# A mixer and MLP trunk on one core: adaLN transposes and ones-matmuls one step later, fewer adaLN steps in the mLSTM output gate

## The chip, the cores and the metric

The kernel runs on one core of one Trainium2 chip. The metric is device time in microseconds for one execution, the median of several. The core's engines are TensorE (PE), VectorE (DVE), ScalarE (ACT), GpSimd (POOL) and SyncE (SP), which here issues nearly all DMAs.

## What is computed

A trunk of two layers over x of 512 rows by 1024 columns, in float32. Layer 0 mixes with an mLSTM, layer 1 with a gated MLP (SGU); each mixer is followed by a squared-ReLU MLP (FFN0 and FFN1 below). Every sub-layer is wrapped by a normalisation whose scale, shift and gate come from a conditioning vector c:

```python
c_act = jax.nn.silu(c)
for i in range(DEPTH):
    mod = c_act @ ada_w[i] + ada_b[i]
    sh1, sc1, g1, sh2, sc2, g2 = jnp.split(mod[:, None, :], 6, axis=-1)
    h = rmsnorm(x, norm_g[i, 0]) * (1.0 + sc1) + sh1
    y = mlstm_mixer(...) if i % N_MIXERS == 0 else sgu_mixer(...)
    x = x + g1 * rmsnorm(y, norm_g[i, 1])
    h = rmsnorm(x, norm_g[i, 2]) * (1.0 + sc2) + sh2
    y = jnp.square(jax.nn.relu(h @ ffn_w1[i])) @ ffn_w2[i]
    x = x + g2 * rmsnorm(y, norm_g[i, 3])
```

The mLSTM computes h @ w_in into queries, keys, values, an output gate o and two gates per head; 128-row chunks then give scores (q k times a decay matrix), mixed values, a state that runs through the chunks, a head norm, and the product with sigmoid(o), which goes through w_out.

## The kernel before, in words

All large products are three float32r matmuls each: weights are loaded raw into a ring of three 16 KB-per-partition buffers (raw), ScalarE casts the high part (whi), VectorE subtracts for the low part (wlo), and `mm3` multiplies hi by hi, hi by lo and lo by hi. A unit of work is 24 such matmuls of 128x512 into one PSUM bank. The stages run in this order: q and gates, k, v (two column halves of four units, `cb`), then the output gate `o_unit` mixed with scores, keys, mixed, state and gated by a list in the code, then `out_proj` (two halves), then FFN0 and so on.

Beside this, each sub-layer prepares the adaLN numbers of its own gate g and of the next normalisation (ab) from ada_w, in small steps that the generator of `Prep` hands out: `prep.step()` stands behind most units. `ada_g` makes g in two halves s of 512 columns; each half reads two raw blocks (g1 to g4 below), sums them on VectorE into an R buffer r, casts the sum into hi and lo (buffers t), and multiplies them by a matrix of ones on TensorE into the PSUM tile pa, which sums over the partitions. `ada_ab` makes the eight column blocks of scale and shift, ab0 to ab7: two loads, two ScalarE products to begin the sums, six VectorE sums, one POOL addition that merges two partial sums (`ada_merge`), two TensorE transposes into pa (`ada_tr`), and one reduction with three small operations on VectorE (`ada_fin`). pa has one bank, R two buffers, raw three, and the weights' whi and wlo four each.

In the mLSTM, the decay matrices of two chunks at a time (`decay`) are read back from a small DRAM tensor dm by DMA, get a mask (capm) on POOL, and go through sixteen exponentials on ScalarE. Eight more reads of dm scale the queries.

Up to the q projection the instructions are kept in the program's order; after it a scheduler orders each engine's instructions by its own estimate, within what the data and the buffers allow. DMAs on SP go out in their order, and an issue whose buffer is still in use holds all behind it. A table of moved transposes (`places`, `behind`) belongs to the end of a sub-layer and is not touched. The rows carry one line number, that of the helper that records every instruction (L50), so tiles name the work. The steps concerned are:

```python
        def steps(self, gate, nxt):
            yield from ada_g(self, *gate)
            if nxt is not None:
                for k in range(KC):
                    self.ab.append(ada_ab(*nxt, k))
                    yield
```

Of the kernel before, what the change touches and what calls it, by code (L numbers as in the profile page):

```python
# [19 lines left out]
KC = D // P  # L20
# [13 lines left out]
def trunk(ctx: ExitStack, tc: tile.TileContext, x, c, norm_g, ada_w, ada_b, ffn_w1, ffn_w2,  # L34
# [62 lines left out]
    def f32(t):  # L97
        return t.bitcast(F32)
# [54 lines left out]
    def ada_load(l, vs, vc, k):  # L153
        raw = rp.tile([P, KC, 2, P], F32, tag="raw", name=nm("raw"))
        w = ada_w[l].rearrange("(k p) f -> p k f", p=P)
        for i, v in enumerate((vs, vc)):
            ld.dma_start(raw[:, :, i, :], w[:, :, v * D + k * P:v * D + (k + 1) * P])
        return raw
# [12 lines left out]
    def ada_merge(acc):  # L171
        pool.tensor_add(acc[:, 0], acc[:, 0], acc[:, 1])

    def ada_tr(acc, merge=True):
        if merge:
            ada_merge(acc)
        ps = bank3()
        for i in range(2):
            pe.transpose(out=ps[:, i * P:(i + 1) * P], in_=acc[:, 0, i * P:(i + 1) * P], identity=ident)
        return ps  # L180
# [7 lines left out]
        dve.tensor_mul(ab[:, 1:2], ab[:, 2:3], ngcol(l, ng, k))  # L188
        return ab[:, 1:2], ab[:, 0:1]

    def ada_ab(l, vs, vc, ng, k):

        raw = ada_load(l, vs, vc, k)
        acc = R().rearrange("p (c i f) -> p c (i f)", c=2, i=2)
        ada_init(raw, acc)
        ada_acc(raw, acc, range(6))
        return ada_fin(ada_tr(acc), l, vs, vc, ng, k)

    def ada_g(box, l, v, ng):

        g = gp.tile([P, D], F32, tag="g", name=nm("g"))
        box.g = g
        w = ada_w[l].rearrange("(k p) f -> p k f", p=P)
        for s in range(2):
            f0 = v * D + s * S
            acc = R()
            pool.memset(acc, 0.0)
            ld.dma_start(acc[0:1, :], ada_b[l:l + 1, f0:f0 + S])
            for hf in range(2):
                raw = rp.tile([P, 4, S], F32, tag="raw", name=nm("raw"))  # L210
                ld.dma_start(raw, w[:, hf * 4:hf * 4 + 4, f0:f0 + S])
                for j in range(4):
                    kk = hf * 4 + j
                    dve.scalar_tensor_tensor(out=acc, in0=raw[:, j], scalar=cact[:, kk:kk + 1],
                                             in1=acc, op0=ALU.mult, op1=ALU.add)
                yield
            ngb = R()
            ld.dma_start(ngb, norm_g[l, ng:ng + 1, s * S:(s + 1) * S].broadcast_to([P, S]))
            ps = bank3()
            hi, lo = T(F32R), T(F32R)  # L220
            act.copy(hi, acc)
            dve.tensor_sub(lo, acc, f32(hi))
            pe.matmul(ps, lhsT=ones, rhs=hi, start=True, stop=False)
            pe.matmul(ps, lhsT=ones, rhs=lo, start=False, stop=True)
            dve.tensor_mul(g[:, s * S:(s + 1) * S], ps, ngb)
            yield


    def conv(raw_ap, scale=None, lo_eng=None):
# [207 lines left out]
    def mlstm(h, prep, after):  # L437
# [37 lines left out]
        pt = bank2()  # L475
        for i in range(2):
            pe.transpose(out=pt[:, i * P:(i + 1) * P], in_=pk[:, i, :], identity=ident)
        aps = ada_tr(accs_[0])
        xn = []
        for t in range(NT):  # L480
# [43 lines left out]
        raws.append(ada_load(0, 0, 1, 2))  # L524
        load_q(2)
        ada_start(2)
        aps = ada_tr(accs_[1])
        xps = xT(1)
        for k in range(KC):
            if k + 2 < KC:  # L530
                ada_acc(raws[k + 2], accs_[k + 2], range(6))
            if k + 1 < KC:
                ab.append(ada_fin(aps, 0, 0, 1, 0, k + 1))
            if k + 3 < KC:
                raws.append(ada_load(0, 0, 1, k + 3))
                load_q(k + 3)
                ada_start(k + 3)
            if k + 2 < KC:
                ada_merge(accs_[k + 2])
            if k + 1 < KC:  # L540
                feed(k + 1, xps, pool)
                q_hi(k + 1)
                q_lo(k + 1)
            hh, hl = h(k, slice(0, S))
            mm3(accs[0], wgc[k // 4][0][:, k % 4], wgc[k // 4][1][:, k % 4], hh, hl, k == 0, k == KC - 1)
            for f in range(4):
                fs = slice(f * P, (f + 1) * P)
                mm3(accs[1 + f], qw[k][0][:, fs], qw[k][1][:, fs], hh, hl, k == 0, k == KC - 1)
            if k + 2 < KC:
                aps = ada_tr(accs_[k + 2], False)  # L550
                xps = xT(k + 2)
        kblk = w_cols(w, 512)
        pinned[0] = False
# [152 lines left out]
        def o_unit(cb, t):  # L706
            if t == 0:
                oblk[0] = w_rows(w, 0, 2048 + cb * S) + w_rows(w, 4, 2048 + cb * S)
            ps = bank()
            proj_tm(ps, oblk[0], h, t)  # L710
            o = A()
            act.activation(o, ps, AF.Sigmoid)
            so[t][cb] = o
            if cb or t > 1:
                prep.step()

        sts = [A(shape=(P, 2, DV + 1)) for _ in range(2)]
# [280 lines left out]
    class Prep:  # L998
# [6 lines left out]
        def steps(self, gate, nxt):  # L1005
            yield from ada_g(self, *gate)
            if nxt is not None:
                for k in range(KC):
                    self.ab.append(ada_ab(*nxt, k))
                    yield  # L1010

        def step(self, n=1):
            for _ in range(n):
# [50 lines left out]
```

## Time and profile before

| | us |
|---|---|
| median of 3 runs (1287.57 to 1288.25) | 1287.77 |
| the profiled execution | 1290.01 |
| its span on the core | 1288.3 |
| TensorE busy in the span | 1234.9 |
| VectorE / ScalarE / POOL busy | 675.9 / 523.4 / 238.7 |
| mean granted TensorE clock, of full | 0.993 |

TensorE sets the time, so one looks for the stretches in which it stands still, and for those in which it runs at the lower of its two clock levels. A timeline gives each group of instructions its start and length, and in brackets the idle time before it and the engine and tile that ended that idle time.

### The profile page before, as it was taken

The page shows a single profiled execution, that of the slowest core. Times are in us where ns is not written, and L with a number is a line of the kernel's source. Part 1 is how long each engine was busy: PE and PEld are TensorE (multiplying, and loading weights), DVE is VectorE, ACT ScalarE, POOL GpSimd, SP SyncE. Part 2 cuts the span into 40 slices and gives each one's busy share as a digit, 9 for nine tenths or more (in the row PEclk, how much of TensorE's full clock was granted, in tenths as well). Part 3 has the DMA queues.
Part 4 walks back from the last instruction along what each step waited for, and adds up shares of the span by engine and source line. Part 5 has one row for each costly group of instructions (what it writes and reads, how often), then busy time and mean ns, then how long its engine had stood idle before and what let it go on. Part 6 is the DMA issues. An engine that isn't in the chain of part 4 may idle for free.

```text
span 1288.3 us, 15197 instructions
## 1 busy us (share of the span) xinstructions
PE 1234.9 (96%) x5849; PEld 1016.5 (79%) x5849; DVE 675.9 (52%) x1124; ACT 523.4 (41%) x923; POOL 238.7 (19%) x230
## 2 busy tenths in 40 slices
PE   3899998999999999999999999999999999999997
PEld 2677777888788888888778888888887888888886
DVE  5796677476853343323786766623566222333225
ACT  4544535384433243413563644323653321343221
POOL 5601311013420022200120023200122200122000
PEclk9999999999999999999999999999999999999999
DMA  9846842424862442222367555322255214332201
GB/s 271 232 165 193 269 111 98 131 89 149 226 199 103 134 134 96 98 98 78 126 203 251 160 153 147 108 99 69 95 165 171 98 66 131 99 98 98 98 33 66
DMA packets 165610, 174.25 MB, mean 135 GB/s; under 512 B 6168, under 2 KB 120936, under 8 KB 165536
## 3 DMA queue, kind: packets, MB, share of 16 engines
q1 hardware_dynamic: 165408, 173.17, 42.8%
q8 instruction: 46, 0.75, 0.2%
q14 instruction: 28, 0.23, 0.1%
q0 software_dynamic: 128, 0.09, 0.0%
HBM read 171.11 MB, written 2.14 MB: 134 GB/s over the span
## 4 chain that ended last, share of the span: by engine, by line
PE 66%; DVE 4%; ACT 2%; POOL 1%; issue 1%; DMA 1%; DVEq 0%; POOLq 0%; ACTq 0%
PE ps L50 64%; PE pt L50 1%; POOL s L50 1%; DVE wlo L50 1%; DVE r L50 1%; DVE x L50 1%; ACT j L50 1%; DVE a L50 1%; DMA raw<-in_ada_w 1%; PE pa L50 0%; ACT whi L50 0%; ACT t L50 0%; POOL r L50 0%; DVE hlo L50 0%; DVE t L50 0%
## 5 line engine op out<-in xcount | busy, mean ns | idle before, releaser
L50 PE MATMUL ps<-whi,a 128*128 128x512 f32 x1408 | 438.5, 391 | 0.0
L50 DVE TENSOR_TENSOR wlo<-raw,whi 128x1024 fp32r<-128x1024 f32 x196 | 241.9, 1238 | 313.8 <-ACT whi L50 304.1
L50 ACT CAST whi<-raw 128x1024 fp32r<-128x1024 f32 x196 | 205.1, 1051 | 285.7 <-PE ps L50 250.2
L50 PEld LDWEIGHTS ps<-whi,a 128*128 128x128 f32 x1408 | 265.0, 188 | 54.8 <-PE pa L50 0.2
L50 PE MATMUL ps<-hlo,whi 128*128 128x512 f32 (+1 forms) x744 | 277.4, 373 | 3.0 <-POOL hlo L50 3.0
L50 PE MATMUL ps<-hhi,whi 128*128 128x512 f32 (+1 forms) x744 | 279.2, 375 | 0.6 <-ACT whi L50 0.6
L50 PE MATMUL ps<-hhi,wlo 128*128 128x512 f32 (+1 forms) x744 | 277.4, 373 | 0.7 <-DVE wlo L50 0.7
L50 PE MATMUL ps<-wlo,a 128*128 128x512 f32 x704 | 274.7, 390 | 0.0
L50 DVE SCALAR_TENSOR_TENSOR r<-raw,cact,r 128x256 f32<-128x256 f32 (+1 forms) x256 | 147.9, 617 | 29.4 <-ACT r L50 17.7
L50 PEld LDWEIGHTS ps<-hlo,whi 128*128 128x128 f32 x744 | 140.4, 189 | 28.2 <-POOL hlo L50 4.1
L50 PEld LDWEIGHTS ps<-hhi,wlo 128*128 128x128 f32 x744 | 140.3, 189 | 25.6 <-DVE wlo L50 1.5
L50 PEld LDWEIGHTS ps<-hhi,whi 128*128 128x128 f32 x744 | 140.4, 189 | 24.2 <-ACT whi L50 1.0
L50 POOL TENSOR_TENSOR t<-t 128x512 f32<-128x512 f32 x64 | 96.7, 1511 | 317.8 <-ACT t L50 317.8
L50 PEld LDWEIGHTS ps<-wlo,a 128*128 128x128 f32 x704 | 132.5, 188 | 27.0
L50 PE MATMUL ps<-wlo,hhi 128*128 128x512 f32 x256 | 101.5, 397 | 3.2 <-DVE wlo L50 3.0
L50 PE MATMUL ps<-whi,hhi 128*128 128x512 f32 x256 | 102.7, 402 | 1.3 <-ACT whi L50 1.3
L50 POOL TENSOR_TENSOR s<-s,mhalf 128x1 f32<-128x1 f32 (+1 forms) x40 | 33.9, 847 | 376.8 <-DVE s L50 369.5
L50 PE MATMUL ps<-whi,hlo 128*128 128x512 f32 x256 | 101.1, 395 | 0.4 <-DVE hlo L50 0.4
L50 DVE TENSOR_TENSOR a<-t,a 128x512 fp32r<-128x512 f32 x64 | 44.2, 691 | 75.5 <-ACT a L50 74.3
L50 ACT CAST a<-t 128x512 fp32r<-128x512 f32 x64 | 39.8, 622 | 101.6 <-POOL t L50 101.6
L50 POOL TENSOR_TENSOR r<-r 128x256 f32<-128x256 f32 x32 | 34.2, 1070 | 183.7 <-DVE r L50 142.5
L50 PEld LDWEIGHTS ps<-wlo,hhi 128*128 128x128 f32 x256 | 48.7, 190 | 15.4 <-DVE wlo L50 5.8
(128 smaller groups left out, 978.8 us busy)
## 6 DMA issues: line engine op xcount, KB each, us to landing
raw<-in_ffn_w SPq DMA_DIRECT2D x64, 1024.0 KB, 5.4
raw<-in_ada_w SPq DMA_DIRECT2D x64, 512.0 KB, 5.6
raw<-in_ada_w SPq DMA_DIRECT2D x16, 1024.0 KB, 5.1
raw<-in_b_w_in SPq DMA_DIRECT2D x16, 1024.0 KB, 5.5
raw<-in_a_w_in SPq DMA_DIRECT2D x10, 1024.0 KB, 5.2
raw<-in_b_w_out SPq DMA_DIRECT2D x8, 1024.0 KB, 6.8
raw<-in_a_w_out SPq DMA_DIRECT2D x4, 1024.0 KB, 5.1
x<-in_x SPq DMA_DIRECT2D x4, 512.0 KB, 7.5
```

The source lines that it names most:

```text
L50: r = f(*a, **k)
```

## The change

Three things are rearranged. In `ada_ab` the transposes and the final small operations of block k come in step k+1, behind the sums and the merge of block k and ahead of the loads of block k+1; it takes nine steps instead of eight. In `ada_g` the second half of the sums no longer ends a step: the cast into hi and lo stands in the same step as the sums, and the ones-matmuls open the next one; it takes four steps instead of six. And the output gate takes a step behind two of its eight units (t == 3) instead of six, so that the remaining steps fall to `out_proj`, whose first half already called `prep.step()` behind each unit.

```diff
-    def ada_tr(acc, merge=True):
-        if merge:
-            ada_merge(acc)
+    def ada_tr(acc):
         ps = bank3()
...
-    def ada_ab(l, vs, vc, ng, k):
-
-        raw = ada_load(l, vs, vc, k)
-        acc = R().rearrange("p (c i f) -> p c (i f)", c=2, i=2)
-        ada_init(raw, acc)
-        ada_acc(raw, acc, range(6))
-        return ada_fin(ada_tr(acc), l, vs, vc, ng, k)
+    def ada_ab(box, l, vs, vc, ng):
+        acc = None
+        for k in range(KC + 1):
+            ps = ada_tr(acc) if k else None
+            if k < KC:
+                raw = ada_load(l, vs, vc, k)
+                acc = R().rearrange("p (c i f) -> p c (i f)", c=2, i=2)
+                ada_init(raw, acc)
+                ada_acc(raw, acc, range(6))
+                ada_merge(acc)
+            if k:
+                box.ab.append(ada_fin(ps, l, vs, vc, ng, k - 1))
+            yield
...
-                yield
+                if hf == 0:
+                    yield
             ngb = R()
             ld.dma_start(ngb, norm_g[l, ng:ng + 1, s * S:(s + 1) * S].broadcast_to([P, S]))
-            ps = bank3()
             hi, lo = T(F32R), T(F32R)
             act.copy(hi, acc)
             dve.tensor_sub(lo, acc, f32(hi))
+            yield
+            ps = bank3()
             pe.matmul(ps, lhsT=ones, rhs=hi, start=True, stop=False)
             pe.matmul(ps, lhsT=ones, rhs=lo, start=False, stop=True)
             dve.tensor_mul(g[:, s * S:(s + 1) * S], ps, ngb)
-            yield
...
+        ada_merge(accs_[0])
         aps = ada_tr(accs_[0])
...
-            if cb or t > 1:
+            if t == 3:
                 prep.step()
...
-                for k in range(KC):
-                    self.ab.append(ada_ab(*nxt, k))
-                    yield
+                yield from ada_ab(self, *nxt)
```

The scheduler then places the DMAs and the engines' instructions anew. On SP, around the second half of the v weights, the order before is as follows. raw from in_a_w_in is a block of v weights (later of o weights), raw from in_ada_w 128x4x512 is a g block and 128x8x128 an ab block, and a from dm 128x4x128 is a decay read.

```order
L50 DMA a_1062<-dm 128x4x128
L50 DMA a_1069<-dm 128x4x128
L50 DMA a_1076<-dm 128x4x128
L50 DMA a_1083<-dm 128x4x128
L50 DMA raw_1137<-in_ada_w 128x4x512
L50 DMA r_1170<-in_norm_g 128x512
L50 DMA raw_1207<-in_ada_w 128x8x128 x2
L50 DMA raw_1256<-in_ada_w 128x8x128 x2
L50 DMA a_1278<-dm 128x4x128
L50 DMA a_1285<-dm 128x4x128
L50 DMA a_1292<-dm 128x4x128
L50 DMA a_1299<-dm 128x4x128
```

The last g block (raw_1137) and norm_g went out behind the first four decay reads, and the second four behind ab0 and ab1; the two v blocks (raw_1090, raw_1100) stood side by side nine rows further up. After the change SP has, from the same four decay reads on:

```order
L50 DMA a_1074<-dm 128x4x128
L50 DMA a_1081<-dm 128x4x128
L50 DMA a_1088<-dm 128x4x128
L50 DMA a_1095<-dm 128x4x128
L50 DMA raw_1112<-in_a_w_in 128x4x512
L50 DMA raw_1153<-in_ada_w 128x8x128 x2
L50 DMA raw_1196<-in_ada_w 128x8x128 x2
L50 DMA raw_1245<-in_ada_w 128x8x128 x2
L50 DMA raw_1294<-in_ada_w 128x8x128 x2
L50 DMA a_1313<-dm 128x4x128
L50 DMA a_1320<-dm 128x4x128
L50 DMA a_1327<-dm 128x4x128
```

The second v block (raw_1112) has the place behind the decay reads, the last g block has moved up to the others, ahead of the first v block, norm_g stands two rows ahead of the decay reads, and the second set of them comes behind two more ab blocks.

On ScalarE, at the end of the v projection, the order before the o weights' casts (whi_1329 to whi_1343) is the following; a<-a,a are the exponentials of decays 2 and 3, a<-ps the copies of v units.

```order
L50 ACTIVATE a_1292<-a_1292,a_849 128x128
L50 COPY a_858<-ps_1180 128x2x128
L50 COPY a_859<-ps_1180 128x2x128
L50 ACTIVATE a_1292<-a_1292,a_849 128x128 x3
L50 ACTIVATE a_1299<-a_1299,a_849 128x128 x4
L50 CAST whi_1329<-raw_1327 128x1024
L50 CAST whi_1333<-raw_1327 128x1024
L50 COPY a_861<-ps_1229 128x2x128
L50 COPY a_862<-ps_1229 128x2x128
L50 CAST whi_1339<-raw_1337 128x1024
L50 CAST whi_1343<-raw_1337 128x1024
```

The second pair of casts stood behind the copies of the last v unit (a_861, a_862). After the change ScalarE has, with the o weights as whi_1364 to whi_1378:

```order
L50 ACTIVATE r_1297<-raw_1294,cact 128x256 x2
L50 ACTIVATE a_1313<-a_1313,a_849 128x128 x4
L50 ACTIVATE a_1320<-a_1320,a_849 128x128 x4
L50 COPY a_861<-ps_1264 128x2x128
L50 COPY a_862<-ps_1264 128x2x128
L50 ACTIVATE a_1327<-a_1327,a_849 128x128 x4
L50 ACTIVATE a_1334<-a_1334,a_849 128x128 x4
L50 CAST whi_1364<-raw_1362 128x1024
L50 CAST whi_1368<-raw_1362 128x1024
L50 CAST whi_1374<-raw_1372 128x1024
L50 CAST whi_1378<-raw_1372 128x1024
```

The last copies of the v projection (a_861, a_862) stood behind the first o casts and now stand ahead of the last eight exponentials, and all o casts behind those.

On TensorE, the end of the second v unit (ps_1143) of this column half and the start of the third (ps_1180) before, with the second ones-matmuls of g between them:

```order
L50 MATMUL ps_1143<-whi_1106,hhi_123 128x512
L50 MATMUL ps_1143<-wlo_1107,hhi_123 128x512
L50 MATMUL ps_1143<-whi_1106,hlo_125 128x512
L50 MATMUL pa_1172<-t_1173,ones 128x512
L50 MATMUL pa_1172<-t_1174,ones 128x512
L50 MATMUL ps_1180<-whi_1092,hhi_122 128x512
```

TensorE went through the units one by one, each with the first half of the v weights (whi_1092, whi_1096) and then the second (whi_1102, whi_1106). After the change, where the second half (whi_1114, wlo_1115) is first used:

```order
L50 MATMUL ps_1215<-wlo_1109,hhi_122 128x512
L50 MATMUL ps_1215<-whi_1108,hlo_124 128x512
L50 MATMUL ps_1122<-whi_1114,hhi_123 128x512
L50 MATMUL ps_1166<-whi_1114,hhi_123 128x512
L50 MATMUL ps_1215<-whi_1108,hhi_122 128x512
L50 MATMUL ps_1215<-wlo_1109,hhi_122 128x512
L50 MATMUL ps_1215<-whi_1108,hlo_124 128x512
L50 MATMUL ps_1122<-wlo_1115,hhi_123 128x512
```

The ones-matmuls stand 19 matmuls further up. Three units now run on the first half of the weights as far as they can; before, each unit took both halves in turn.

## Rows read from the trace of the kernel before

**Rows 1.** page: busy us by engine (share of span), the chain that ended last

```profile
PE 1234.9 (96%) x5849; PEld 1016.5 (79%) x5849; DVE 675.9 (52%) x1124; ACT 523.4 (41%) x923; POOL 238.7 (19%) x230
...
PE 66%; DVE 4%; ACT 2%; POOL 1%; issue 1%; DMA 1%; DVEq 0%; POOLq 0%; ACTq 0%
```

**Rows 2.** TensorE's waits: releaser, us in total, times, longest

```profile
PE pa L50 <- POOL r L50: 8.1, 3, 5.4
...
PE pa L50 <- ACT t L50: 2.7, 1, 2.7
...
PE pa L50 <- DVE t L50: 1.1, 4, 0.5
```

**Rows 3.** timeline of TensorE, 123.6 to 128.8: start, us, operation [idle before <-releaser]

```profile
128.07 0.79 PE L50 MATMUL pa<-t,ones 128*128 128x512 f32 x1 [2.67 <-ACT t L50]
```

**Rows 4.** windows: length, busy us of each engine (instructions), granted clock, DMA share, GB/s

```profile
113.40:125.40 12.00, 12.00 (x53) 9.60 (x52) 5.39 (x8) 8.04 (x22) 6.13 (x4) 1.00 0.89 263
125.40:134.30 8.90, 6.24 (x15) 4.63 (x15) 7.57 (x17) 2.97 (x7) 0.53 (x1) 0.62 0.75 210
143.20:154.00 10.80, 9.52 (x65) 7.77 (x66) 10.61 (x20) 6.58 (x11) 0.81 (x1) 1.00 0.74 204
```

**Rows 5.** timeline of VectorE, 108 to 160

```profile
109.10 0.69 DVE L50 TENSOR_TENSOR g<-pa,r 128x512 f32<-128x512 f32 x1 [2.15 <-PE pa L50]
...
124.26 3.11 DVE L50 SCALAR_TENSOR_TENSOR r<-raw,cact,r 128x512 f32<-128x512 f32 x4 [6.58 <-DMA raw<-in_ada_w]
...
130.72 4.04 DVE L50 SCALAR_TENSOR_TENSOR r<-raw,cact,r 128x256 f32<-128x256 f32 x10
```

**Rows 6.** SP's DMA issues in time, 85 to 133

```profile
104.52 8.77 SPq L50 DMA_DIRECT2D a<-dm  x12
113.38 0.85 SPq L50 DMA_DIRECT2D raw<-in_ada_w  x1
...
126.45 4.00 SPq L50 DMA_DIRECT2D a<-dm  x4
```

**Rows 7.** page, DMA issues: KB each, median us from issue to landing

```profile
raw<-in_a_w_in SPq DMA_DIRECT2D x10, 1024.0 KB, 5.2
```

**Rows 8.** timelines of POOL (110 to 150) and ScalarE (108 to 130)

```profile
133.77 2.14 POOL L50 TENSOR_TENSOR a<-a,capm 128x512 f32<-128x512 f32 x1 [10.86 <-DMA a<-dm]
...
122.95 1.28 ACT L50 ACTIVATE a<-a,a 128x128 f32<-128x128 f32 x4 [0.32 <-POOL a L50]
```

**Rows 9.** timeline of ScalarE, 128 to 155

```profile
142.29 1.98 ACT L50 CAST whi<-raw 128x1024 fp32r<-128x1024 f32 x2
144.17 0.63 ACT L50 COPY a<-ps 128x256 f32<-128x256 f32 x2
```

**Rows 10.** timeline of TensorE, 143 to 156

```profile
150.62 0.50 PE L50 MATMUL ps<-wlo,hhi 128*128 128x512 f32 x1 [1.28 <-DVE wlo L50]
...
151.88 1.95 PE L50 MATMUL ps<-a,a 128*128 128x129 f32 x16
153.76 1.10 PE L50 MATMUL pt<-a,a 128*64 128x129 f32 x16
```

**Rows 11.** timeline of TensorE in the output gate, the rows with idle time

```profile
185.95 0.50 PE L50 MATMUL ps<-wlo,hhi 128*128 128x512 f32 x1 [1.42 <-DVE wlo L50]
...
203.52 0.63 PE L50 MATMUL pt<-ident,a 128*128 128x128 f32 x4 [0.96 <-DVE ab L50]
...
223.35 0.87 PE L50 MATMUL pt<-ident,a 128*128 128x128 f32 x3 [0.68 <-DVE ab L50]
```

**Rows 12.** timeline of TensorE in FFN0, rows of pa

```profile
339.63 0.44 PE L50 MATMUL pa<-ident,r 128*128 128x128 f32 x2 [1.44 <-POOL r L50]
...
352.66 0.44 PE L50 MATMUL pa<-ident,r 128*128 128x128 f32 x2 [1.26 <-POOL r L50]
```

**Rows 13.** FFN0: timelines of ScalarE (a unit's Relu) and VectorE (lo parts)

```profile
345.59 0.60 ACT L50 ACTIVATE t<-ps 128x512 f32<-128x512 f32 x1 [1.15 <-PE ps L50]
...
342.49 2.35 DVE L50 TENSOR_TENSOR wlo<-raw,whi 128x1024 fp32r<-128x1024 f32 x2
```

More of the change, by code (lines that the diff above doesn't have):

```diff
@@ L526, in mlstm @@
         ada_start(2)
+        ada_merge(accs_[1])
         aps = ada_tr(accs_[1])
@@ L549, in mlstm @@
             if k + 2 < KC:
-                aps = ada_tr(accs_[k + 2], False)
+                aps = ada_tr(accs_[k + 2])
                 xps = xT(k + 2)
```

## The prediction

> **What bounds the kernel now.** I read first the busy times and the chain of waits, then TensorE's waits by releaser, then the timelines of the stretches in which TensorE stands still. TensorE is busy 96% of the span and 66% of the chain that ended last is its own [rows 1]. Every matmul of before is still done, so the change can only move TensorE's idle time and its clock. The tile pa, in which the adaLN steps transpose and sum, makes it wait 8.1 us on POOL's merge of r, 2.7 us on ScalarE's t and 1.1 us on VectorE's t [rows 2]. The longest of the three POOL waits, 5.4 us, is the start-up, where the change only moves the merge call. What is at stake directly is then 2.7 + 2.7 + 1.1 = 6.5 us of idle time and what a dropped clock adds. All else is a question of what the new order of loads and casts puts in the way.
>
> **Part 1: the gate sum in the v projection (a gain).** TensorE stops at 125.4 for 2.67 us, for the second ones-matmul of g [rows 3]. Its sum is late because its last raw block, g4, is issued at 113.38, behind twelve reads of dm, and VectorE can start on it only at 124.26 [rows 5, 6]. Behind the stop the granted clock is 0.62 of full: the window of 8.90 us holds 15 matmuls, while the 12.00 us before it held 53 at clock 1.00, 0.226 us each [rows 4]. 15 x 0.226 = 3.4, so the stop costs 8.9 - 3.4 = 5.5 us, 2.7 idle and 2.8 at the half-rate level. After the change g1 to g4 are all issued ahead of the first v block of the second column half, the hi/lo is made one step ahead of its matmuls, and this cost goes: -5.5.
>
> **Part 2: the v block that gave up its place (a loss of about the same size).** The second half of those v weights (v1b) was issued with the first, well ahead; now it stands behind dm, norm_g and four decay blocks on SP's queue. norm_g waits for a buffer that VectorE's product for g frees at 109.8 [rows 5]; with it, two reads of dm and four decay reads ahead, seven issues at 0.73 us (8.77 for twelve [rows 6]), v1b goes out at about 114.9, in the place where g4 was. The nearest row is g4 itself, 10.9 us from 113.38 to 124.26; what then went out behind it, norm_g, now lies ahead, so v1b lands at 125 to 126. On ScalarE its cast stands behind the sixteen exponentials of the first two decays, whose last four began at 122.95 and took 1.28 [rows 8]; with their reads about 1.2 us later (norm_g's wait) they end at about 125.4, and the cast (1.0, as those in rows 9) at 126.5. TensorE has 33 matmuls and the ones pair to do without v1b, where it had 48 before its stop: 13 fewer x 0.226 = 2.9, so it is dry at 122.5. A stop of 4.0 us (3.4 if the reads come no later than before) and the same 2.8 us of slow clock give +6.8. Parts 1 and 2 together: +1.3, and the v stage ends at about 144.4 instead of 143.2.
>
> First the trace on the clock: a stop of 2.67 us was followed by the lower level, one of 1.28 us [rows 10] was not (1.00 in the window around it [rows 4]). The Trainium skill (TensorE: Matmul & The Clock Gate, Part 1) says that the chip's activity window runs freely and does not restart with the kernel's work, so that equal stops may cost unequal slow stretches. By the trace the slow part is 2.8; by that page it could as well be none of it or more, and the sum would move by up to 2.8 either way. I keep the row's value.
>
> **Part 3: the first output-gate unit (a loss).** Before, ScalarE cast its weights from 142.29, without idle time behind the last exponentials of decays 2 and 3 [rows 9]. Now two more ada blocks, ab2 and ab3, are loaded ahead of those decay reads. ab3 needs the buffer that ab0's six sums give back: v1b's second cast ends at 127.5, its lo parts at 128.9, six sums of 0.4 [rows 5] at 131.4. So the reads go out near 133 instead of 126.45 [rows 6]. By the old distance, 7.3 us from the first issue to POOL's first add at 133.77 [rows 6, 8], four adds of 1.3 and a last set of exponentials of 1.3, they end at about 147. ScalarE's own order gives the same: the copies of the last v unit (144.4 + 0.6), then eight exponentials at 0.32 (1.28 for four [rows 8]), is 147.6. Four casts of 1.0 follow, VectorE's four lo parts at 1.2 with small work between them end at about 153.8, and six matmuls then remain: o0 ends near 155.2 (before 151.88 [rows 10]). Ahead of it TensorE has only scores, keys and a quarter of mixed and state; the rest, 12/16 of 1.95 and 13/16 of 1.10 [rows 10], 2.3, follows to about 157.5 against 154.9. So v and o0 together are 2.6 us late, 1.3 of them from here. Bounds: -4 if reads and exponentials come early, +5.4 if the new short stops drop the clock once more for the same 2.8.
>
> **Part 4: the rest of the output gate (a gain).** Of its six steps two stay, and the last three of the shorter list run in the output projection. An ab step issues two DMAs, two ScalarE initialisations, six VectorE sums, a POOL merge, a transpose pair and four small VectorE operations; all of these count again in the output projection, where the transposes' 0.2 to 0.4 us a pair are the same work for TensorE, and merges are a unit old when they are read, so nothing waits. What goes is VectorE's crowding: TensorE waits 1.42 at 185.95 for a lo cast that stands behind such small operations, and 0.96 and 0.68 at 203.52 and 223.35 behind ab itself [rows 11]. I take -1.4 and half of the other two, -0.8; the waits for a that lie between them are the head norm's own and stay. If the cover in the projection failed, its three pairs would show stops of FFN0's size, 1.3 each. The last two blocks of w_out go out behind ab6 and ab7, but half a projection (96 matmuls, 21.7 us) ahead of their use.
>
> **Part 5: FFN0 (a gain, partly given back).** Two transposes stop TensorE for 1.44 and 1.26 waiting for POOL's merge [rows 12]: 2.7 us, gone when they come a unit (24 x 0.226 = 5.4 us) later. But every W1 block is now queued behind two more ada blocks. Before, the first lo part of one pair was made by 343.7 (342.49 and half of 2.35), 1.6 to 1.9 us before the unit ahead of it was through (its Relu starts at 345.59) [rows 13]. With lower leads on three pairs I count 0.9 of the 2.7 as lost, 0.3 a pair: -1.8. Bounds: -2.7, and +1 if each of three pairs comes 1.3 late.
>
> **Part 6: FFN1 and the SGU.** FFN1's preparation has no ab; the ones pairs waited 1.1 us in four times for VectorE's t, 0.5 at most [rows 2], of which half is counted here: -0.6. The SGU has no stop on pa beyond what rows 2 count; its loads trade places as in FFN0. Zero, between -0.5 and +1.
>
> **The sum.** +2.6 (parts 1 to 3) - 1.4 - 0.8 (part 4) - 1.8 (part 5) - 0.6 (part 6) = -2.0 us. The profiled execution took 1290.0 (span 1288.3 and 1.7 around it), 2.2 above the median of 1287.77; 1290.0 - 2.0 = 1288.0 there, and 1285.8 as a median.
>
> **The rivals.** A, the forecast: the stop at 125 is swapped for one at 122.5, the late stages gain 4.6. 1284 to 1288, chance 0.55.
> B: decays and v1b come early, the 5.5 us is won. For it: much less is queued at 114 than before, since g4 is done, and the median block of these weights lands 5.2 us after its issue [rows 7], which puts v1b at 120.1. Against it: the exponentials stand ahead of the cast whenever v1b lands, and these waited for POOL's adds already [rows 8]. Even then o0 still waits for the second decays, so v and o0 end about 2.4 early instead of 2.6 late: 1285.8 - 5 = 1281. Chance 0.17. The Trainium skill (DMA: Bandwidth & Descriptors, Queues, rings and completion order) says that each DMA engine takes descriptors in ring order; by that rule v1b cannot overtake the reads of dm ahead of it, and g4's row agrees.
> C, slower: the stops at 122.5 and in o0 each bring a slow stretch, because they lie some 20 us apart and TensorE starts the second with several short waits in 5 us. That adds 2.8 to A; with the W1 blocks late in FFN0 (+1 instead of -1.8) it is 1285.8 + 5.6 = 1291.4. A second stretch that costs over 2.0 turns the sign by itself. Chance 0.17.
> D: it doesn't do what it says: transposes wait for the same merges one unit later since VectorE's sums wait for later loads, FFN0 gains nothing and the output gate little. 1287.5 to 1288. Chance 0.11.
>
> **How the numbers follow.** A measurement of this kernel tells 0.2%, 2.6 us, from no change: faster means below 1285.2, slower above 1290.3. A puts about 0.24 of its 0.55 below 1285.2 and the rest within; B 0.16 below; C 0.14 above; D within. That is 0.40, 0.46 and 0.14. The range for 8 in 10 goes from B's 1281 to between A and C, 1290.5.
>
> **What would show it.** Right: no stop on pa at 125; a stop of 3 to 4.5 us at about 122.5 that ends with the first cast of v1b, a clock near 0.6 behind it; the o weights' cast from about 147.5; no wait on POOL's r in FFN0. Wrong: TensorE runs through 122 (B); a clock below 1.00 between 145 and 158, or waits on whi or wlo at FFN0's odd units (C); pa waits that only moved (D).

## The result: 8 us slower, most of it in a stage that the prediction had set to zero

The changed kernel takes 1295.63 us (1293.58 to 1297.11, four runs) against 1287.67 for the kernel before; the ratio is 1.0065 with a 95% interval of 1.0045 to 1.0086, some 8 us more. I had forecast 1285.8, with 1281.0 to 1290.5 as the range. The sign was wrong and the range did not hold the time.

The profiled executions differ by 7.1 us (spans 1295.4 and 1288.3), about what the medians do, so the two traces can be compared stretch by stretch, within the play of single executions that is given below the table. I cut both at the same work: the transposes behind the q stage, the first scores, the first matmul of the second output-gate unit, and the first matmuls of FFN0, SGU and FFN1. These are windows of the kernel before (length, busy us of TensorE, its weight loads, VectorE, ScalarE and POOL with their instructions, granted clock, DMA share, GB/s):

```profile
89.94:143.16 53.22, 50.47 (x216) 39.95 (x216) 35.29 (x69) 26.50 (x69) 14.34 (x23) 0.94 0.69 213
143.16:154.79 11.63, 10.35 (x78) 8.43 (x77) 11.40 (x26) 7.40 (x14) 0.81 (x1) 1.00 0.76 218
154.79:275.19 120.40, 113.54 (x637) 92.47 (x635) 79.46 (x217) 57.41 (x153) 15.79 (x17) 0.99 0.35 108
275.19:624.53 349.34, 344.98 (x1603) 286.51 (x1603) 161.30 (x225) 126.11 (x186) 62.54 (x46) 1.00 0.43 135
624.53:929.02 304.49, 301.60 (x1432) 248.65 (x1432) 181.93 (x314) 144.25 (x265) 51.34 (x47) 1.00 0.45 139
929.02:1288.30 359.28, 350.48 (x1622) 292.12 (x1622) 138.52 (x154) 119.41 (x172) 53.28 (x39) 0.99 0.31 104
```

And of the changed kernel:

```profile
88.26:142.98 54.72, 50.52 (x218) 40.26 (x218) 40.38 (x85) 22.47 (x56) 9.80 (x22) 0.94 0.66 197
142.98:160.45 17.47, 13.41 (x80) 10.94 (x79) 11.12 (x26) 13.83 (x37) 4.53 (x4) 0.80 0.91 303
160.45:275.67 115.22, 110.89 (x632) 90.22 (x631) 75.49 (x202) 55.16 (x142) 14.60 (x16) 1.00 0.30 94
275.67:624.55 348.88, 345.09 (x1603) 286.58 (x1603) 163.20 (x225) 125.94 (x186) 63.38 (x46) 1.00 0.42 135
624.55:935.60 311.05, 304.58 (x1433) 249.36 (x1433) 179.07 (x314) 144.16 (x265) 53.51 (x47) 0.99 0.44 137
935.60:1295.40 359.80, 349.99 (x1622) 292.18 (x1622) 137.24 (x154) 119.45 (x172) 52.99 (x39) 0.99 0.31 103
```

The lengths in the second block less those in the first give the ledger:

| stretch | measured, us | predicted, us |
|---|---|---|
| up to the q transposes (same order in both) | -1.7 | 0 |
| k and v projections | +1.5 | +1.3 |
| first output-gate unit (o0) with scores, mixed, state | +5.8 | +1.3 |
| rest of the output gate, output projection | -5.2 | -2.2 |
| FFN0 | -0.5 | -1.8 |
| SGU | +6.6 | 0 |
| FFN1 | +0.5 | -0.6 |

The measured column compares one execution of each kernel, and the traces of the experiments below lend it a scale, since each keeps the old steps in some sub-layers. With the old steps, k and v took 52.0 to 54.8 us in eight traces, k and v together with the first output-gate unit 64.0 to 65.2, the rest of the gate 119.0 to 120.5; FFN0 took 348.2 to 349.3 and FFN1 359.3 to 359.9 in eleven traces, the SGU 304.4 to 305.3 in seven. The changed kernel has 54.7, 72.2, 115.2, 348.9, 359.8 and 311.1. So the first output-gate unit, the rest of the gate and the SGU stand clear of the play, and the other rows do not. The -1.7 of the first row is chance: the trace of the kernel before has a clock of 0.83 between 50 and 60 us, that of the changed kernel 1.00, and such a slow stretch stands in the start-up of six of the fourteen traces.

Idle time is the length less TensorE's busy time. More busy time for the same matmuls can be a lower clock, but need not be: the trace of the SGU alone, below, has more of it at a clock of 1.00. In the SGU idle time goes from 2.89 to 6.47 and busy time from 301.60 to 304.58. Of these 3.0 us the clock can make 1.7, the 17% that it lacks in the ten us from the stop on:

```profile
736.34:746.34 10.00, 9.47 (x33) 7.35 (x34) 8.73 (x19) 8.89 (x17) 1.10 (x2) 0.83 0.36 116
```

In the first output-gate unit there are 2.8 us more of idle time and 3.1 of busy time, at a clock of 0.80 against 1.00. The same two levels (1.2 and 2.4 GHz) show as mean clocks between 0.5 and 1 in windows that hold both.

TensorE's waits in the changed kernel (releaser, us in total, times, longest), which answer [rows 2]:

```profile
PE ps L50 <- ACT whi L50: 9.7, 6, 4.1
...
PE pa L50 <- POOL r L50: 7.0, 2, 5.4
PE pa L50 <- ACT t L50: 1.6, 1, 1.6
```

The waits for pa behind the start-up fell from 6.5 us to 3.2 (1.6 for r and 1.6 for t), so half of them went, as the change means them to. What came in their place is waiting for casts of weights: whi 9.7 us in six stops, against 1.8 in three before.

**The v stage.** TensorE's timeline in the changed kernel, then the end of the exponentials and the cast on ScalarE, and SP's issues:

```profile
124.97 1.65 PE L50 MATMUL ps<-whi,hhi 128*128 128x512 f32 x3 [4.11 <-ACT whi L50]
```

```profile
122.57 1.28 ACT L50 ACTIVATE a<-a,a 128x128 f32<-128x128 f32 x4 [1.49 <-POOL a L50]
123.87 1.99 ACT L50 CAST whi<-raw 128x1024 fp32r<-128x1024 f32 x2
```

```profile
112.10 1.36 SPq L50 DMA_DIRECT2D raw<-in_a_w_in  x1
113.55 20.39 SPq L50 DMA_DIRECT2D raw<-in_ada_w  x8
133.99 4.13 SPq L50 DMA_DIRECT2D a<-dm  x4
```

No wait on ones is left here, and in the place of [rows 3] there is a stop of 4.11 us for the displaced v block's cast, which follows the last exponentials without idle time. The clock was 0.66 in the 10.15 us from 120.85 on. The four ab blocks take SP until 133.99, when the second decay reads go out ([rows 6]: 126.45).

**The first output-gate unit.** TensorE, POOL and ScalarE:

```profile
146.34 0.44 PE L50 MATMUL pa<-ident,r 128*128 128x128 f32 x2 [1.61 <-POOL r L50]
...
149.81 0.79 PE L50 MATMUL ps<-whi,hhi 128*128 128x512 f32 x1 [2.45 <-ACT whi L50]
```

```profile
141.34 4.26 POOL L50 TENSOR_TENSOR a<-a,capm 128x512 f32<-128x512 f32 x3 [1.60 <-DMA a<-dm]
145.56 0.73 POOL L50 TENSOR_TENSOR r<-r 128x256 f32<-128x256 f32 x1
```

```profile
147.55 1.28 ACT L50 ACTIVATE a<-a,a 128x128 f32<-128x128 f32 x4 [0.16 <-POOL a L50]
148.73 1.98 ACT L50 CAST whi<-raw 128x1024 fp32r<-128x1024 f32 x2
```

The o weights' cast begins at 148.73 instead of 142.29 [rows 9], behind the last exponentials. A stop that I had not counted lies ahead of it: the transposes of ab3 come before state on TensorE, and the merge that they wait for stands on POOL behind three mask additions, which wait for the late decay reads. Two stops, 1.61 and 2.45 us within 5.1 us of time, and the clock falls (0.66 in the ten us from 146 on). The first of them takes no time of its own: the cast that ends at 149.76 sets the start of o0 either way, and without the wait for the merge TensorE would have waited longer for the cast.

**The SGU.** TensorE, ScalarE and VectorE near the end of the v projection:

```profile
736.34 0.50 PE L50 MATMUL ps<-hhi,whi 128*128 128x512 f32 x1 [1.31 <-ACT whi L50]
737.60 0.50 PE L50 MATMUL ps<-hhi,wlo 128*128 128x512 f32 x1 [0.53 <-DVE wlo L50]
```

```profile
735.26 1.03 ACT L50 CAST whi<-raw 128x1024 fp32r<-128x1024 f32 x1
```

```profile
722.61 0.69 DVE L50 TENSOR_TENSOR a<-ps,a 128x512 f32<-128x512 f32 x1 [0.62 <-DMA a<-in_b_b_in]
```

The u weights' first cast stands on ScalarE behind squares of the v part's norm, with no idle time before it, and these follow from VectorE's sum of the first unit of the last v block with its bias, which waited for the bias itself to be read. Some 55 us ahead of this stop there are two waits that the kernel before does not have:

```profile
676.79 0.66 PE L50 MATMUL pt<-ident,a 128*128 128x128 f32 x4 [0.82 <-POOL a L50]
683.62 0.55 PE L50 MATMUL pt<-ident,a 128*128 128x128 f32 x3 [0.70 <-POOL a L50]
```

These transposes wait for a mask addition on POOL, and that for a read of in_b_ws. The two reads go out on SP at 670.5 and 675.1, behind the first loads of ab blocks; before, they went out at 668.0 and 672.3, ahead of all ab loads. Counted from the SGU's start, TensorE is some 2 us later than in the kernel before when it comes to the stop at 736.

### The profile page after: what moved, and what is told of

Read it like the earlier page. It is cut to its first block, busy times and chain, and to the rows that moved or that the text cites. A ratio compares the mean times of both kernels' runs of the same rounds, so it can differ in the third digit from the quotient of the medians.

```text
span 1295.4 us, 15195 instructions
## 1 busy us (share of the span) xinstructions
PE 1237.3 (96%) x5849; PEld 1017.0 (79%) x5849; DVE 675.2 (52%) x1124; ACT 523.5 (40%) x923; POOL 239.4 (18%) x230
## 4 chain that ended last, share of the span: by engine, by line
PE 68%; DVE 14%; DMA 6%; ACT 5%; POOL 3%; issue 3%; SPq 1%; POOLq 0%; DVEq 0%; ACTq 0%
PE ps L50 66%; DVE r L50 5%; DVE a L50 4%; DVE wlo L50 3%; DMA raw<-in_ada_w 3%; ACT j L50 2%; PE pt L50 2%; POOL s L50 2%; DVE x L50 1%; DMA a<-in_b_ws 1%; ACT whi L50 1%; ACT t L50 1%; DMA a<-in_b_b_in 1%; DMA a<-in_b_bs 1%; DVE s L50 1%
## 5 line engine op out<-in xcount | busy, mean ns | idle before, releaser
L50 PEld LDWEIGHTS ps<-whi,hhi 128*128 128x128 f32 x256 | 49.2, 193 | 19.1 <-ACT whi L50 8.9
```

The lines of the kernel that those rows point to most:

```text
L50: r = f(*a, **k)
```

## The experiments

The comparisons are ratios to the kernel before on the same chip; microseconds are these ratios times 1287.7. In all of them the new and the old steps live in one program, and a number for the sub-layer (0 mLSTM, 1 FFN0, 2 SGU, 3 FFN1) chooses:

```diff
         def steps(self, gate, nxt):
-            yield from ada_g(self, *gate)
+            yield from (ada_g2 if self.i in G else ada_g)(self, *gate)
             if nxt is not None:
+                if self.i in AB:
+                    yield from ada_ab2(self, *nxt)
+                    return
                 for k in range(KC):
                     self.ab.append(ada_ab(*nxt, k))
                     yield
```

`ada_g2` and `ada_ab2` are the changed kernel's steps.

### Which sub-layer pays

**The mLSTM alone** (G = AB = {0}, with the changed output-gate condition).

> The new steps in the mLSTM alone, the old ones in the other three sub-layers. Theory (each sub-layer pays by its own order): the two traces, set to zero at the transposes behind the q stage, differ by +2.2 us when FFN0 begins, so +2 us (+1 to +4) on the median; TensorE stops for about 4 us behind the first v block and about 4 us ahead of the first output-gate unit, both with a slow stretch behind, and nothing stops it for over 0.6 us in the SGU's v projection. Rival (the mLSTM's two slow stretches are the whole loss, and the SGU only suffers from what comes to it late): +6 to +8 us.

Measured: 1.0019 (1.0009 to 1.0029), +2.4 us. The stops are those of the changed kernel:

```profile
125.19 0.96 PE L50 MATMUL ps<-whi,hhi 128*128 128x512 f32 x3 [3.91 <-ACT whi L50]
...
146.07 0.44 PE L50 MATMUL pa<-ident,r 128*128 128x128 f32 x2 [2.16 <-POOL r L50]
...
149.54 0.80 PE L50 MATMUL ps<-whi,hhi 128*128 128x512 f32 x1 [2.44 <-ACT whi L50]
```

Nothing stopped TensorE in the SGU's v projection here beyond what it does before. The theory holds: the mLSTM's two slow stretches are paid, and most of the loss is won back in the rest of the output gate.

**FFN0 alone** (G = AB = {1}).

> The new steps in FFN0 alone. Theory: the two waits on POOL's merge (1.44 and 1.26 us) go and waits for the cast of W1 blocks of about the same sum come: -0.5 us (-1.5 to +1). Rival (the cast waits come from the mLSTM's steps, which leave the buffers to FFN0 in another state): no cast waits, -2.5 us.

Measured: 1.0006 (0.9996 to 1.0015), +0.8 us (-0.5 to +1.9). Waits for pa on POOL are gone, and these came:

```profile
331.95 0.50 PE L50 MATMUL ps<-hhi,wlo 128*128 128x512 f32 x1 [1.35 <-DVE wlo L50]
...
344.27 0.50 PE L50 MATMUL ps<-hhi,wlo 128*128 128x512 f32 x1 [0.66 <-DVE wlo L50]
```

The first is within 0.1 us of the stop that it replaces (1.44 in [rows 12]). The theory's mechanism is shown; the size is a shade worse than its -0.5, though within its range.

**The SGU alone** (G = AB = {2}).

> The new steps in the SGU alone. Theory: the SGU's loss of 6.6 us between the two traces is made in the SGU by its own order, so +6.5 us (+4.5 to +8), with TensorE waiting for a cast of ScalarE near the end of the v projection and a granted clock near 0.6 behind that. Rival (it comes from what FFN0 hands on): within 1.5 us of before.

Measured: 1.0047 (1.0031 to 1.0063), +6.1 us. The stop is there with nothing else changed:

```profile
735.19 0.50 PE L50 MATMUL ps<-hhi,whi 128*128 128x512 f32 x1 [1.38 <-ACT whi L50]
736.45 0.50 PE L50 MATMUL ps<-hhi,wlo 128*128 128x512 f32 x1 [0.53 <-DVE wlo L50]
```

Its granted clock is not that of the changed kernel. It stayed at 1.00 in the ten us from the stop on, and in the whole SGU:

```profile
735.19:745.19 10.00, 9.47 (x41) 7.54 (x42) 8.73 (x20) 8.78 (x17) 1.10 (x2) 1.00 0.32 108
```

Still the SGU took 309.9 us, 4.6 to 5.4 more than with the old steps. So the theory is right on the place and wrong on the clock near 0.6: the SGU makes the larger part of the loss by its own order, and a slow stretch is no necessary part of it.

**FFN1 alone** (G = {3}).

> The new steps in FFN1 alone; it prepares only g. Theory: +0.4 us (-0.5 to +1), one wait for ScalarE's t of about 1.6 us in place of two short ones. Rival (the ones-matmuls a step later need not wait): -0.6 us.

Measured: 0.9999 (0.9990 to 1.0008). No difference that can be told, though the wait of about 1.6 us for t is there (1.58 in this trace); it is too little to show. The four ratios add up to +0.71%, the change as a whole measured +0.65%: the sub-layers pay separately.

### The mLSTM: what takes the gain

**The second v block first.** Its loads and casts are written ahead of the step behind the first half's last unit:

```diff
+                if cb == 0 and t == 3:
+                    vblk = w_rows(w, 0, 1024 + S) + w_rows(w, 4, 1024 + S)
                 prep.step()
```

> The new steps in the mLSTM alone, and the loads and casts of the second half of the v weights written ahead of the step behind the first half's last unit, so that both blocks again stand ahead of the last g block. Theory (the v block that lost its place on SP's queue makes the first stop, and o0's stop comes from the second decays): the stop at 121 to 125 and its slow stretch go, the waits ahead of o0 stay or grow, -3 us against e1_mlstm, so -1.5 to +0.5 us against before. Rival (o0's casts set the time of both, the v stage only waits sooner): as e1_mlstm, +2.5 us.

Measured: 1.0004 (0.9994 to 1.0014), +0.5 us, so some 2 us under the mLSTM alone; the intervals of the two overlap a little. The stop at 121 is gone, and so is one slow stretch. But another took its place:

```profile
131.82 0.69 PE L50 MATMUL pa<-ident,r 128*128 128x128 f32 x2 [3.94 <-POOL r L50]
...
147.47 0.65 PE L50 MATMUL pt<-a,a 128*64 128x129 f32 x6 [1.44 <-DVE a L50]
...
149.06 0.50 PE L50 MATMUL ps<-whi,hhi 128*128 128x512 f32 x1 [0.93 <-ACT whi L50]
```

The block's place made the first stop, as the theory says; with it mended, the transposes of ab0 wait 3.94 us for a merge, since TensorE still comes to them earlier than before. The waits ahead of o0 fell from 4.6 to 2.4 us instead of staying, which the theory had not expected.

**The output-gate condition alone** (G and AB empty).

```diff
-            if cb or t > 1:
+            if t == 3:
                 prep.step()
```

> Only the condition in the mLSTM's output gate is changed (a step behind two units instead of six). Theory (the late output gate's gain, 5.2 us between the two traces from the end of o0 to FFN0, comes from the steps that left it): -3 us (-1.5 to -5), with the stop at 125 as before. Rival (it comes from the lag of the transposes): within 1 us of before.

Measured: 0.9990 (0.9981 to 1.0000), -1.3 us, at the interval's edge. The theory's sign holds, its size doesn't: TensorE still has the wait of 1.42 for a lo part that I had put on VectorE's ab work, and one at the head norm has grown:

```profile
183.72 0.50 PE L50 MATMUL ps<-wlo,hhi 128*128 128x512 f32 x1 [1.42 <-DVE wlo L50]
191.27 0.63 PE L50 MATMUL pt<-ident,a 128*128 128x128 f32 x4 [1.09 <-DVE s L50]
```

**Each load where it was.** The new steps are two fewer ahead of the first ab block, so a step is left out at two units of the v projection (t = 2 of the first half, t = 1 of the second), and one is added to the output gate:

```diff
-                prep.step()
+                if t != 2 - cb:
+                    prep.step()
...
-            if t == 3:
+            if t == 3 or (cb == 1 and t == 1):
                 prep.step()
```

> The new steps in the mLSTM alone, taken at six of the eight places of the v projection so that each g and ab block is loaded where it was before, and at three units of the output gate. Theory (the loss is the loads brought forward; the lag and the lighter output gate are a gain): the stop behind the first v block and the long ones ahead of o0 are gone, a stop for the second half of g's sum near 125 may stay in another form since that block lands late again, -2 us against before (-4 to 0). Rival (the lag costs in the v projection, because pa is held longer): 0 to +3 us.

Measured: 0.9965 (0.9955 to 0.9976), -4.5 us, 1283.73 us: faster than both kernels. The load order on SP is that of the kernel before up to the o weights, the transposes keep their lag. There is no stop over 0.25 us between the q transposes and 136.9; the one for the o weights is there earlier and costs a slow stretch:

```profile
141.61 0.80 PE L50 MATMUL ps<-whi,hhi 128*128 128x512 f32 x1 [4.69 <-ACT whi L50]
```

So the new steps, the lag with them, are a gain in the mLSTM: 3 us of it are left when the 1.3 of the output gate's condition are taken off. What lost it was that a shorter list of steps at unchanged places asks for every load earlier.

### The SGU: what makes the stop

**Bias rows read ahead.**

```diff
+        bbs = []
+        for cb in range(4):
+            bb = A()
+            ld.dma_start(bb, b_b_in[0:1, GH + cb * S:GH + (cb + 1) * S].broadcast_to([P, S]))
+            bbs.append(bb)
         for cb in range(4):
-            bb = A()
-            ld.dma_start(bb, b_b_in[0:1, GH + cb * S:GH + (cb + 1) * S].broadcast_to([P, S]))
+            bb = bbs[cb]
```

> The new steps in the SGU alone, as e3_sgu, and the four bias rows of the v projection read together at its start instead of each ahead of its weights. Theory (the last bias read stands on SP behind two weight blocks that wait for a buffer, VectorE adds it late, and ScalarE's casts stand behind what hangs on that): the stop of 1.4 and 0.5 us at about 735 and its slow stretch go, -4.5 us against e3_sgu, +1.5 us against before (0 to +3). Rival (the casts are late because of the weights themselves or of ScalarE's order): as e3_sgu, +6 us.

Measured: 1.0044 (1.0028 to 1.0060), +5.7 us, the same as without. VectorE no longer waits for a bias and ScalarE's first cast of u weights is no longer the last wait, but TensorE stops as long as before, now for the lo part:

```profile
734.19 0.50 PE L50 MATMUL ps<-hhi,wlo 128*128 128x512 f32 x1 [1.77 <-DVE wlo L50]
```

My theory fell. The late bias was a wait on the way that cost nothing by itself: behind it the next one was as late.

**The lag without the shorter g steps** (G empty, AB = {2}).

> Only the transposes' lag of the ab steps in the SGU; the g steps as before. Theory (the order of SP's loads decides, and it changes because the shorter g steps bring the ab loads forward): SP's order in the v projection is that of before, and the time too, within 1 us. Rival (the lag itself costs): +3 to +6 us.

Measured: 1.0015 (1.0005 to 1.0025), +1.9 us: neither. SP's order in the v projection is that of before and the stop at 735 is absent, so the lag isn't what makes it; but the time is over the 1 us that I allowed, and one transpose pair waits in the u part:

```profile
835.17 0.41 PE L50 MATMUL pa<-ident,r 128*128 128x128 f32 x2 [1.59 <-DVE s L50]
```

pa has one bank, and VectorE reads the block before it only behind a lo part that begins at 832.32 and one more sum:

```profile
834.62 0.41 DVE L50 TENSOR_REDUCE s<-pa 128x2 f32<-128x256 f32 x1
```

**Each load where it was**, in the SGU.

```diff
-                if i in (0, 1, 3, 4, 6, 7, 9, 10):
+                if i in (0, 1, 4, 6, 9, 10):
                     prep.step()
...
-            if gg in (3, 6, 9, 12, 14):
+            if gg in (1, 3, 6, 9, 12, 14):
                 prep.step()
```

> The new steps in the SGU alone, taken at six of the eight places of the v projection (behind units 0, 1, 4, 6, 9, 10) and one more in the u part, so that each load goes out where it did before; the lag of transposes and ones-matmuls stays. Theory (the loss of e3_sgu is that the shorter list brings two more ab blocks into the v projection, with their loads, sums and buffers ahead of what the u weights need): within 1 us of before, no stop for a cast near 735. Rival (the lag itself or the shorter g step costs): +4 to +6 us as e3_sgu.

Measured: 1.0011 (1.0002 to 1.0020), +1.4 us. The stop of 735 is gone (its place has one of 0.62), and with it three quarters of the loss. Up to the first u weights the loads are where they were, two ab blocks ahead of them; behind these the third and the fourth ab block go out earlier than before, by one weight block and by two.

**Only the last two steps taken out** (units 0, 1, 3, 4, 6, 7; the u part as in the one before).

> The new steps in the SGU alone, without the last two of the eight steps in the v projection (behind units 9 and 10), which are made up for by one step in the u part and one at its end: the loads of g and of the first two ab blocks stay brought forward, the next two go behind the v projection's weights. Theory (it is the two added ab blocks ahead of the last v and the first u weights that make the stop near 735): as s_match, +1.5 us (0 to +3), no stop over 0.8 us near 735. Rival (the earlier g and ab blocks, which put the third v block's weights behind them, cost): +4 to +6 us as e3_sgu.

Measured: 1.0013 (1.0004 to 1.0023), +1.7 us, as in the run before. TensorE at that point:

```profile
732.12 0.50 PE L50 MATMUL ps<-hhi,wlo 128*128 128x512 f32 x1 [0.62 <-DVE s L50]
```

So the stop at 735, and with it most of the SGU's loss, comes from the two ab blocks that the shorter list added to the end of the v projection. Whether they hurt by their buffers (each takes one of three raw buffers until its sums are done) or by their sums on VectorE, ahead of the norm's, isn't told apart by these runs. Of the last 1.7 us the trace shows a part: the two transposes that wait for in_b_ws still do so here, 0.62 and 1.00 us, as the first ab loads stay brought forward. In the run before these two waits are gone, and what its last 1.4 us is stays open.

### All four, with the loads where they were

G = AB = all, with the step places of the two.

> The change in all four sub-layers with the steps of s_match and m_match. Theory: the sum of the parts, -2 (m_match) + 0.7 (e2_ffn0) + 0 (s_match, e4_ffn1), so -1.3 us against before (-4 to +1) and some 9 us under the changed kernel. Rival (the lag costs by itself): +2 us or more.

Measured: 0.9990 (0.9981 to 0.9999), -1.3 us, and by the ratios 9.7 us under the changed kernel. Taken over the four sub-layers the new steps no longer cost, though the lag does in the SGU (+1.9 alone, +1.4 with moved steps). In FFN0 the wait for casts is still there, 1.18 and 0.69 in this trace, with a clock of 0.83 in the window from 326 to 336. The mLSTM alone, with its loads in place, is the fastest version that was run, 3.2 us ahead of this one; FFN0 and the SGU, which cost 0.8 and 1.4 by themselves, make 2.2 of that.

## Why the prediction was wrong, by its steps

**Part 1 and 2 (the v stage): right, place by place.** Read from the q transposes on, the changed kernel's trace is 1.7 us early, so its 120.85 is my 122.5 (predicted 122.5), its stop 4.11 us (4.0), the end of the exponentials 125.5 (125.4), and the stage is 1.5 us later (1.3). That the length agrees to 0.2 us is partly luck, as this stage took 52.0 to 54.8 us with the old steps. When the weights landed is not shown: their cast followed the exponentials without idle time. So no run shows that they stayed behind the reads of dm, as the prediction holds against rival B.

**Part 3 (the first output-gate unit): the mechanism right, the term mis-sized, 5.8 in place of 1.3.** Two things were off. ScalarE's casts began at 148.73, which is 150.4 on the prediction's scale, where I had 147.6: SP was held by the four ab blocks until 133.99 (135.7, where I had 133), the decay reads went out that much later, and the exponentials ahead of the casts ended later with them. And I kept the second slow stretch as a bound, 2.8 us, and as rival C with 0.17; it came, and busy time grew by 3.1. I had also let TensorE run scores, keys and the transposes of ab3 without a wait, though that merge stands on POOL behind mask additions whose reads I had just moved 7 us. After two stops of 1.6 and 2.5 us so close together the row of 1.28 us that had kept its clock was the wrong neighbour; the row of 2.67 us was the nearer one.

**Part 4 (the rest): sign and idle time right (2.5 against 2.2), 5.2 gained in all, the other half by busy time that I had not counted.** In the kernel before a slow stretch follows the last two stops at about 222 (the later one is in [rows 11]):

```profile
222.00:232.00 10.00, 9.32 (x39) 7.59 (x38) 8.06 (x16) 1.79 (x3) 0.00 (x0) 0.83 0.30 101
```

It makes up to 1.7 of the 2.65 us less of busy time; the window also holds five matmuls fewer. It is absent from the changed kernel's trace and from that of the mLSTM alone, but also from one of the eight with the old steps, so that the change removes it is likely and not shown. The condition alone gave 1.3 us, and the wait of 1.42 for a lo part that I had given to it stayed in that run; in the changed kernel it is 0.82.

**Part 5 (FFN0): the step that failed is "0.3 a pair".** The displaced W1 block was late in two places:

```profile
334.22 0.50 PE L50 MATMUL ps<-hhi,wlo 128*128 128x512 f32 x1 [1.38 <-DVE wlo L50]
346.35 0.50 PE L50 MATMUL ps<-hhi,wlo 128*128 128x512 f32 x1 [0.47 <-DVE wlo L50]
```

The stops for a merge became stops for a lo part, to within 0.1 us at the first. The gain to be had was smaller than I said, too: of the two stops of [rows 12] the second is absent from other traces with the old FFN0, that of the mLSTM alone among them. I had the lead (1.6 us) in [rows 13], and the block's issue falls behind two more loads; that no lead of this size survives is what the row should have said. FFN0 has the size of rival D and the late W1 blocks of rival C.

**Part 6 (the SGU): the step that failed and decides the sign.** I set it to zero with the words that its loads trade places as in FFN0, and worked out no chain there, because rows 2 show no wait on pa. I looked where the change takes waits away, and not at what it moves forward. The change shortens the list of steps from 14 to 13 and the g part from 6 to 4, at unchanged places: by the end of the v projection four ab blocks are loaded where it was two. The diff shows that, and so do SP's issues ahead of the first u weights. With it a stop of 1.3 + 0.5 us at the end and 1.7 us more of other short ones follow, and 3.0 us more of busy time, of which a slow stretch can make 1.7: 6.6 us in this trace. The experiments put 4.4 of the 6.1 us that the SGU alone cost on those two blocks (1.0047 against 1.0013).

**Rival C** named the mechanism of the mLSTM and of FFN0, two slow stretches and casts late, and gave 1291.4; the SGU, which no rival named, makes the rest. Its chance was too low: I counted the lower clock as a mishap, where each of the three places with over 1.8 us of stops within a few microseconds had it in the changed kernel's trace. It is no certainty either, since the SGU alone kept its clock behind 1.38 and 0.53 us.

**What the prediction took from the Trainium skill** (TensorE: Matmul & The Clock Gate, Part 1), that equal stops may cost unequal slow stretches, the runs bear out: 1.31 and 0.53 us in the SGU were followed by a clock of 0.83, 1.38 and 0.53 us in the SGU alone by 1.00. I had taken it as a reason to widen by 2.8 us to either side at one place, and it applied to more.

## What to carry to other kernels

When a list of small steps gets shorter and is called from the same places, all that stands behind in the list moves forward; count the loads that come before each weight block in every stage, and not only in the stages where the old waits are. A stop that is taken away on one tile has a successor on the same path: work out who is second, with its queue on POOL and ScalarE, before the gain is booked. A stretch that is read from one execution is a sample: where the same steps run in several traces, take their range before a difference is explained. And where the schedule has moved, put the steps back to where their loads were and measure again: the new steps that lost 2.4 us in the mLSTM alone won 4.5 there once the loads stood in their old places.

## What the runs showed of the hardware

The stop at 125 in the kernel before is not the same from execution to execution. FFN0's experiment has the old program up to there, and TensorE's timeline in it shows four stops instead of one:

```profile
119.31 0.50 PE L50 MATMUL ps<-wlo,hhi 128*128 128x512 f32 x1 [1.10 <-DVE wlo L50]
127.04 0.50 PE L50 MATMUL pa<-t,ones 128*128 128x512 f32 x1 [0.86 <-ACT t L50]
127.77 0.50 PE L50 MATMUL pa<-t,ones 128*128 128x512 f32 x1 [0.23 <-DVE t L50]
135.59 0.44 PE L50 MATMUL pa<-ident,r 128*128 128x128 f32 x2 [1.85 <-POOL r L50]
```

The window around them kept the full clock:

```profile
117.00:140.00 23.00, 18.95 (x82) 14.52 (x81) 13.34 (x24) 12.46 (x38) 11.67 (x9) 1.00 0.93 286
```

4.0 us of stops in 23 us cost 4.0 us there, and one of 2.67 us cost 5.5 in the profiled execution of before. In the eight traces with the old mLSTM the wait for t at this place is between 0.80 and 2.67 us. A term that is read from one execution's slow stretch, as my -5.5, has that much play. I had also not expected that the sub-layers' losses would add so closely (0.71% for the four, 0.65% for all together).
